# The relative-position bias of a two-layer encoder: one small DRAM copy read as overlapping rows, in place of 128 copies per head

## The chip, the cores and the metric

One core of a Trainium2 chip runs the whole program. The metric is device time in microseconds (us) of one execution; lower is better. TensorE (PE in the rows) multiplies matrices, with weight loads shown apart as PEld; VectorE is DVE, ScalarE (the activation engine) is ACT, GpSimd is POOL, and SyncE (SP) issues DMAs. ACT can issue DMAs too: a DMA issued by SP goes to the queue q1 of the profile, one issued by ACT to q10, and both are served by the core's 16 DMA engines.

## The reference, cut to what matters

Layer 0 is differential attention with a T5 relative-position bias and a block-causal mask; layer 1 is forgetting attention; both are followed by a squared-ReLU MLP (256 tokens, 2048 features, float32). The change concerns only the bias of layer 0:

```
rel  = key_pos[None, :] - q_pos[:, None]                  # [128 queries of a block, 256 keys]
bias = transpose(rel_table[t5_bucket(rel)], (2, 0, 1))    # 8 heads
mask = (key_pos[None, :] // 64) <= (q_pos[:, None] // 64)
s    = where(mask, s * scale + bias[None, :, None], -1e30)
p    = softmax(s)
```

The bias depends on the head and on key minus query alone. For the 256 queries and keys there are 383 such differences that the kernel needs (-255 to 127), so a head's bias is one row of 383 numbers, and each query reads a stretch of 256 of them, shifted by one from query to query.

## The kernel before

All products are float32 done as three reduced products: a weight tile `raw` is split into a high part `whi` (a cast on ACT, L171) and a low part `wlo` (a subtraction on VectorE, L174), and PE multiplies both with split operands. The weights come as *granules* of 512 KB, numbered here 0, 1, 2, ... in the order in which PE takes them. One granule is one *slot* of PE: about 2.8 us of matmuls. SP loads granules (L163) into four `raw` buffers; the load of granule i + 4 is issued when the low part of granule i has been taken. Five `whi` and five `wlo` buffers hold what is split, four granules ahead of PE. Each engine runs its instructions strictly in the order in which the program writes them, slot by slot: lists `pre`, `mid` and `post` say what side work stands in which slot.

The first eight slots (granules 0 to 7) make the first value block (L185 to L187), while x is still coming in; slots 8 to 11 make the queries of head 0, slots 12 to 15 its keys (L200, L203), and its scores follow two slots later. In the steady part one granule is taken in each slot.

The bias is made beside this. In slot 5 PE multiplies the table with a one-hot matrix from the host (`bias_rows`, L329) into `bp`: 8 heads by 383 differences. At the start of slot 6 VectorE copies it to `bs` (8 partitions, L333), and SP writes it to DRAM as `F` (L335), each head's row 128 times, 1532 KB in all. In slot 8 SP reads it back (L343) as `T`: 128 query rows by 8 heads by 256 keys, 1024 KB, by reading rows of 383 with a step of 382, so that each query's row begins one number earlier. GpSimd then writes the mask into a corner of `T` (L344). VectorE reads `T` in the softmax of each head (L406):

```
F = dr.tile([NA, P, NREL], F32, tag="F", name="F")
nc.sync.dma_start(out=F, in_=bs[:, 0:NREL].unsqueeze(1).broadcast_to([NA, P, NREL]))
...
src = src.rearrange("h (q r) -> q h r", r=NREL - 1)[:, :, 0:S]
nc.sync.dma_start(out=T, in_=src)
```

The DMA that reads `F` may be issued only once all of `F` has landed; SP waits for that, and its later loads wait behind it.

Of the kernel before, what the change touches and what calls it, by code (L numbers as in the profile page):

```python
# [11 lines left out]
F32 = mybir.dt.float32  # L12
# [8 lines left out]
P = 128  # L21
D = 2048
S = 256
HD = 128
FF = 8192
NA = 8          # differential heads
NF = 16         # forgetting heads
CW = 512        # columns of a token-major unit
# [6 lines left out]
NREL = 383      # rel = -255 .. 127  # L35

LA = 4          # granules split ahead of the products
NRAW = 4        # granules in flight from DRAM
# [4 lines left out]
def kernel(ctx: ExitStack, tc: tile.TileContext, *args):  # L43
# [11 lines left out]
    # ------------------------------------------------------------------ constants  # L55
# [9 lines left out]
    # 1 where a token is up to another: within a block of 128, and a block before  # L65
# [6 lines left out]
    # residual stream, token-major, by chunks of 512 features  # L72
# [6 lines left out]
    # the activation engine's tables come in beside the first loads  # L79
# [3 lines left out]
    # gains as columns: rows of 128 features, transposed  # L83
# [38 lines left out]
    # ------------------------------------------------------------------ the stream of weights  # L122
    # side work by slot of the tensor engine: before its weights' split, amid it, and after the products
    pre, mid, post = (defaultdict(list) for _ in range(3))
    order = []      # (unit, granule, token tiles): what the tensor engine does

    class Gran:
        """Weights of one transfer: kk tiles of 128 rows, 1024 numbers a partition."""
# [4 lines left out]
    class Unit:  # L133
        """One result in two banks: its granules, its operand, and what takes it."""
# [10 lines left out]
    def unit_b(W, r0, nk, c0, xs, done):  # L145
        """[256, 512] = x . W[r0 : r0 + nk * 128, c0 : c0 + 512], token-major."""
        gs = []
        for k in range(0, nk, 2):
            src = W[r0 + k * P:r0 + (k + 2) * P, c0:c0 + CW].rearrange("(k p) c -> p k c", p=P)
            gs.append(Gran(src, 2))  # L150
        return Unit("B", gs, xs, done)

    def unit_a(W, c0, xs, done):
        """[256 features, 256 tokens] = (x . W[:, c0 : c0 + 256]) transposed."""
        gs = []
        for k in range(0, 16, 4):
            src = W[k * P:(k + 4) * P, c0:c0 + 256].rearrange("(k p) c -> p k c", p=P)
            gs.append(Gran(src, 4))
        return Unit("A", gs, xs, done)
# [52 lines left out]
    # ------------------------------------------------------------------ pieces  # L212
    def new_x(tag):
        """Two 128-row tiles of an operand: high parts of 256 tokens, then low parts."""
        return sb.tile([P, 2, 2 * S], F32R, tag=tag, name=tag)

    def turn(c, tps):
        """h[c] feature-major, into two banks."""
        for b in range(2):
            for j in range(2):  # L220
                for m in range(2):
                    f = (2 * b + j) * P
                    nc.tensor.transpose(tps[b][:, (j * 2 + m) * P:(j * 2 + m + 1) * P],  # L223
                                        h[c][:, m, f:f + P], ident)

    def split_turned(c, tps, gain, dst, bs=(0, 1)):
        """High and low parts of gain . h[c] turned, from two pieces of 512 columns."""
        at = [(b, j, 4 * c + 2 * b + j) for b in bs for j in range(2)]
        for b, j, k in at:
            nc.scalar.activation(out=dst[2 * c + b][:, j, 0:S], in_=tps[b][:, j * S:(j + 1) * S],  # L230
                                 func=AF.Copy, scale=gain[:, k:k + 1])
        for b, j, k in at:
            nc.vector.scalar_tensor_tensor(out=dst[2 * c + b][:, j, S:2 * S], in0=tps[b][:, j * S:(j + 1) * S],  # L233
                                           scalar=gain[:, k:k + 1], in1=dst[2 * c + b][:, j, 0:S],
                                           op0=ALU.mult, op1=ALU.subtract)
# [10 lines left out]
    def rsqrt(ssum, n, scale, eps, name, bufs=1):  # L246
        """(ssum * scale + eps) ** -0.5 by columns: three Newton steps from the exponent's half."""
        v = sb.tile([P, n], F32, tag="rs_v", bufs=2, name="rs_v")
        w = sb.tile([P, n], F32, tag="rs_w", bufs=2, name="rs_w")
        t = sb.tile([P, n], F32, tag="rs_t", bufs=2, name="rs_t")  # L250
        y = sb.tile([P, n], F32, tag=name, bufs=bufs, name=name)
        nc.vector.tensor_scalar(out=v, in0=ssum, scalar1=scale, scalar2=eps, op0=ALU.mult, op1=ALU.add)
        nc.vector.tensor_scalar(out=y.bitcast(I32), in0=v.bitcast(I32), scalar1=-0.5,
                                scalar2=1597463007.0, op0=ALU.mult, op1=ALU.add)
        nc.vector.tensor_scalar(out=w, in0=v, scalar1=-0.5, scalar2=None, op0=ALU.mult)
        for _ in range(3):
            for i in range(n):
                c = slice(i, i + 1)
                nc.vector.scalar_tensor_tensor(out=t[:, c], in0=y[:, c], scalar=w[:, c], in1=y[:, c],
                                               op0=ALU.mult, op1=ALU.mult)  # L260
            for i in range(n):
                c = slice(i, i + 1)
                nc.vector.scalar_tensor_tensor(out=y[:, c], in0=t[:, c], scalar=1.5, in1=y[:, c],
                                               op0=ALU.add, op1=ALU.mult)
        return y

    class Norm:
        """Row statistics of the residual stream: rstd by token, and along the free axis."""
# [33 lines left out]
    def pair_sum(u):  # L302
        """The two halves of a feature-major unit's banks added: [128, 2, 256]."""
# [16 lines left out]
    # ------------------------------------------------------------------ prologue: x, T5 bias, lambda  # L320
# [10 lines left out]
    def bias_out():  # L331
        bs = sb.tile([NA, 512], F32, tag="e", bufs=2, name="bs")
        nc.vector.tensor_copy(out=bs[:, 0:NREL], in_=bias["p"][0:NA, 0:NREL])  # L333
        F = dr.tile([NA, P, NREL], F32, tag="F", name="F")
        nc.sync.dma_start(out=F, in_=bs[:, 0:NREL].unsqueeze(1).broadcast_to([NA, P, NREL]))  # L335
        bias["F"] = F

    def bias_in():
        T = sb.tile([P, NA, S], F32, tag="tnc", bufs=2, name="T")
        # T[q, head, j] = F[head, q, 127 - q + j]: rows of 383, read 382 apart  # L340
        src = bias["F"].rearrange("h q r -> h (q r)")[:, 127:127 + P * (NREL - 1)]
        src = src.rearrange("h (q r) -> q h r", r=NREL - 1)[:, :, 0:S]
        nc.sync.dma_start(out=T, in_=src)  # L343
        nc.gpsimd.memset(T[0:64, :, 192:256], NEG)  # L344
        bias["T"] = T

    def build_lambda():
# [7 lines left out]
        # -(e1 - e2 + init)  # L355
# [4 lines left out]
    # ------------------------------------------------------------------ layer 0: differential attention  # L360
# [25 lines left out]
    def diff_head(hd):  # L386
# [13 lines left out]
        def softmax(qt):  # L400
            def run():
# [3 lines left out]
                b = bias["T"][:, hd, S - nk:S].unsqueeze(1).broadcast_to([P, 2, nk])  # L405
# [96 lines left out]
    # boundary after the last product that a chunk of h takes  # L502
# [35 lines left out]
    n_mlp0, n_att1, n_mlp1 = (Norm.__new__(Norm) for _ in range(3))      # started by their first chunk  # L538
# [9 lines left out]
    def wo(W, kind, p0, p1, dones):  # L548
        """h += o . W over the head pairs p0 to p1; the last pair of the first two chunks comes last."""
# [13 lines left out]
    # ------------------------------------------------------------------ squared-ReLU MLP  # L563
    HX = {}

    def mlp(l, norm, key, last, start=None):
        for q in range(4):
# [20 lines left out]
            for c in range(NCH):  # L588
                u = unit_b(w_out[l], q * D, 16, c * CW, lambda hk=hk: HX[hk], adds[c] if q < 3 else last[c])
                if l == 1 and q == 3 and c == NCH - 1:  # L590
                    # the last result: one token tile ends before the other
# [8 lines left out]
    # ------------------------------------------------------------------ layer 1: forgetting attention  # L600
    fg = {}

    def gates(s0):
# [24 lines left out]
        def gate1():  # L628
            # z = logits by token; n = min(z, 0); t = exp(-|z|)
# [15 lines left out]
        def gate2():  # L645
            # log1p(t) = 2 atanh(s), s = t / (2 + t) in [0, 1/3]
# [20 lines left out]
        def gate4():  # L667
            # log sigmoid = min(z, 0) - log1p(exp(-|z|))
# [6 lines left out]
        def sums():  # L675
            # over the tokens up to each: by head and token
# [41 lines left out]
    def spread_c(g):  # L718
        """-c over the keys on every partition, causal on the diagonal blocks: diagonal 0 | full | diagonal 1."""
# [9 lines left out]
    def fox_pair(g, i):  # L729
        """Heads 4 g + 2 i and the next."""  # L730
# [88 lines left out]
    def v_first(s0):  # L819
        """Beside the first unit of layer 1: the forget gates, and the query operand."""  # L820
# [12 lines left out]
    def qkv_f(g):  # L833
# [6 lines left out]
        for i in range(2):  # L840
# [3 lines left out]
            def then(e, plan=plan, i=i):  # L844
                # the last values come after the last queries
# [16 lines left out]
    # ------------------------------------------------------------------ last MLP and the final norm  # L862
# [45 lines left out]
    # ------------------------------------------------------------------ emission  # L908
    grs, at = [], []        # the granules as they come; how many the slots so far have taken
# [22 lines left out]
    # the tensor engine's clock comes up while the first rows are on their way  # L932
# [42 lines left out]
    for s in range(n + 2):  # L975
        for f in pre.pop(s, []):
            f()
        # while x comes in, one granule less is split ahead
# [32 lines left out]
def bucket_onehot():  # L1011
    """Row b, column r: 1 where the T5 bucket of rel = r - 255 is b."""
    rel = np.arange(-255, NREL - 255)
# [29 lines left out]
```

## Time and profile before

| | us |
|---|---|
| median of 3 runs (lowest, highest) | 2267.74 (2267.03 to 2269.26) |
| span of the profiled execution, first to last instruction | 2266.5 |
| median less that span | 1.24 |
| PE busy | 2234.6 (99% of the span) |
| VectorE, ACT busy | 1356.8 (60%), 1022.4 (45%) |
| mean granted TensorE clock | 0.994 of full speed |

The profile gives the profiled execution by its span alone; what lies around it is taken as the 1.24 us between that span and the median. PE is busy nearly always, so the time of this kernel is PE's work plus PE's few idle stretches. A busy share over the whole span says little of a stage: the questions are when PE stands still, and what it then waits for.

### The profile page before, as it was taken

Reading aid. Unit: us, or ns where it says so; the run is one execution under the profiler, and the core shown is the slowest. Engines: PE = TensorE matmul, PEld = TensorE weight load, DVE = VectorE, ACT = ScalarE, POOL = GpSimd, SP = SyncE. Lnnn points to the kernel's source line nnn. Section 1 sums busy time; section 2 is a strip of 40 time slices with the busy share of each in tenths; the row PEclk is TensorE's granted clock in tenths of the full one; section 3 lists DMA queues with packets and bytes.
Section 4 is the critical chain, followed back from the end, with each engine's and each line's share of the span. In section 5 each row is a group of like instructions: output and inputs, shape, how many; then the busy total and the mean of one; then the engine's idle time right before and its main releaser. Section 6 shows DMA issues by size and latency. Waiting matters only on the chain.

```text
span 2266.5 us, 28986 instructions
## 1 busy us (share of the span) xinstructions
PE 2234.6 (99%) x11272; PEld 1874.0 (83%) x11272; DVE 1356.8 (60%) x1768; ACT 1022.4 (45%) x1343; POOL 14.0 (1%) x19
## 2 busy tenths in 40 slices
PE   8799999999999999999999999999999999999998
PEld 6688888888888888888888888888888888888886
DVE  4566665665565565466576556656645655655655
ACT  4454554443444344344554444454434434433443
POOL 0000000000000000000001000000000000000000
PEclk9899999999999999999999999999999999999999
DMA  7655555556556655666556565556565565565563
GB/s 198 200 178 176 159 176 177 171 187 200 180 187 194 191 184 188 187 189 188 170 169 203 175 192 181 178 168 203 186 187 185 186 194 178 186 197 178 187 200 130
DMA packets 319332, 416.06 MB, mean 184 GB/s; under 512 B 15066, under 2 KB 218972, under 8 KB 319068
## 3 DMA queue, kind: packets, MB, share of 16 engines
q1 hardware_dynamic: 319148, 414.20, 58.4%
q8 instruction: 88, 1.44, 0.3%
q14 instruction: 48, 0.39, 0.1%
q10 hardware_dynamic: 48, 0.02, 0.0%
HBM read 410.49 MB, written 3.68 MB: 183 GB/s over the span
## 4 chain that ended last, share of the span: by engine, by line
PE 97%; DMA 2%; DVE 0%; ACT 0%; issue 0%; SPq 0%; DVEq 0%; ACTq 0%
PE acc L200 31%; PE acc L203 16%; PE acc L187 15%; PE acc L185 15%; PE acc L186 15%; DMA raw<-in_w_qkv_a 2%; PE tp L223 1%; PE sc L396 0%; PE sc L739 0%; PE sc L187 0%; PE sc L186 0%; PE sc L185 0%; PE o L797 0%; PE fp L610 0%; PE o L798 0%; PE tpo L474 0%
## 5 line engine op out<-in xcount | busy, mean ns | idle before, releaser
L174 DVE TENSOR_TENSOR wlo<-raw,whi 128x1024 fp32r<-128x1024 f32 x767 | 926.1, 1224 | 646.9 <-ACT whi L171 646.1
L171 ACT CAST whi<-raw 128x1024 fp32r<-128x1024 f32 x767 | 797.3, 1050 | 751.5 <-PE acc L187 460.2
L200 PE MATMUL acc<-x,whi 128*128 128x512 f32 x2816 | 993.8, 399 | 18.7 <-ACT whi L171 18.7
L203 PE MATMUL acc<-x,wlo 128*128 128x256 f32 x2816 | 776.9, 281 | 0.5 <-DVE wlo L174 0.5
L200 PEld LDWEIGHTS acc<-x,whi 128*128 128x128 f32 x2816 | 525.5, 188 | 139.4 <-ACT whi L171 19.0
L203 PEld LDWEIGHTS acc<-x,wlo 128*128 128x128 f32 x2816 | 532.7, 189 | 9.1 <-DVE wlo L174 1.0
L185 PE MATMUL acc<-whi,hx 128*128 128x512 f32 x1120 | 443.4, 396 | 0.0
L187 PE MATMUL acc<-whi,hx 128*128 128x512 f32 x1120 | 442.4, 395 | 0.0
L186 PE MATMUL acc<-wlo,hx 128*128 128x512 f32 x1120 | 442.3, 395 | 0.0
L187 PEld LDWEIGHTS acc<-whi,hx 128*128 128x128 f32 x1120 | 209.9, 187 | 51.3
L186 PEld LDWEIGHTS acc<-wlo,hx 128*128 128x128 f32 x1120 | 210.0, 187 | 51.0
L185 PEld LDWEIGHTS acc<-whi,hx 128*128 128x128 f32 x1120 | 210.0, 187 | 50.5
L307 DVE TENSOR_TENSOR zs<-acc,z 128x512 f32<-128x512 f32 x96 | 66.3, 691 | 102.8 <-ACT z L306 102.8
L306 ACT COPY z<-acc 128x512 f32<-128x512 f32 x96 | 56.4, 587 | 157.1 <-PE acc L200 157.1
L581 ACT CAST hx<-s 128x512 fp32r<-128x512 f32 x64 | 39.8, 622 | 143.2 <-DVE s L579 143.2
L185 PE MATMUL acc<-whi,x 128*128 128x512 f32 x256 | 102.7, 401 | 0.2 <-ACT x L230 0.2
L187 PE MATMUL acc<-whi,x 128*128 128x512 f32 x256 | 100.1, 391 | 0.6 <-DVE x L233 0.6
L186 PE MATMUL acc<-wlo,x 128*128 128x512 f32 x256 | 99.8, 390 | 0.0
L200 PE MATMUL acc<-hx,whi 128*128 128x512 f32 x256 | 92.1, 400 | 0.0
L582 DVE TENSOR_TENSOR hx<-s,hx 128x512 fp32r<-128x512 f32 x64 | 44.3, 693 | 44.0 <-ACT hx L581 44.0
L203 PE MATMUL acc<-hx,wlo 128*128 128x256 f32 x256 | 70.6, 281 | 0.0
L318 DVE TENSOR_TENSOR h<-acc,h 128x512 f32<-128x512 f32 x88 | 56.7, 686 | 17.9 <-PE acc L187 17.8
(172 smaller groups left out, 1170.0 us busy)
## 6 DMA issues: line engine op xcount, KB each, us to landing
raw<-in_w_mlp_in SPq DMA_DIRECT2D x256, 512.0 KB, 3.9
raw<-in_w_mlp_out SPq DMA_DIRECT2D x256, 512.0 KB, 3.8
raw<-in_w_qkv_a SPq DMA_DIRECT2D x96, 512.0 KB, 4.6
raw<-in_w_o_a SPq DMA_DIRECT2D x32, 512.0 KB, 4.2
raw<-in_w_v_b SPq DMA_DIRECT2D x32, 512.0 KB, 3.8
raw<-in_w_k_b SPq DMA_DIRECT2D x32, 512.0 KB, 3.7
raw<-in_w_q_b SPq DMA_DIRECT2D x32, 512.0 KB, 3.8
raw<-in_w_o_b SPq DMA_DIRECT2D x32, 512.0 KB, 3.6
```

Source lines behind the costliest of these rows:

```text
L171: nc.scalar.copy(out=g.hi, in_=g.raw)
L174: nc.vector.tensor_tensor(out=g.lo, in0=g.raw, in1=g.hi, op=ALU.subtract)
L185: nc.tensor.matmul(bank[m], xh, hi[:, j, :], start=k == 0, stop=False)
L186: nc.tensor.matmul(bank[m], xh, lo[:, j, :], start=False, stop=False)
L187: nc.tensor.matmul(bank[m], xl, hi[:, j, :], start=False, stop=k == nk - 1)
L200: nc.tensor.matmul(bank[n], hi[:, j, w], xt, start=k == 0, stop=k == 15)
L203: nc.tensor.matmul(bank[n][:, 0:S], lo[:, j, w], xt[:, 0:S], start=False, stop=False)
L306: nc.scalar.copy(out=z1, in_=u.acc[:, :, S:2 * S])
L307: nc.vector.tensor_tensor(out=zs, in0=u.acc[:, :, 0:S], in1=z1, op=ALU.add)
L318: nc.vector.tensor_tensor(out=h[c][:, m, :], in0=u.bank[m], in1=h[c][:, m, :], op=ALU.add)
L581: nc.scalar.copy(out=t[:, :, 0:S], in_=s)
L582: nc.vector.tensor_tensor(out=t[:, :, S:2 * S], in0=s, in1=t[:, :, 0:S], op=ALU.subtract)
```

## The change

`F` holds each head's row once (8 by 383), with the differences in reversed order, 127 down to -255. It is written by a DMA that ACT issues. `T` is read back, also on ACT's queue, with the step 1 from partition to partition: partition q reads 256 numbers from place q of each head's row, so the rows overlap. What partition q then holds is its bias with the keys in reversed order; VectorE reads it with step -1, and the mask's corner moves from the last 64 columns to the first 64. The one-hot matrix from the host has its columns reversed to suit. The rest of the diff removes comments.

```
     def bias_out():
         bs = sb.tile([NA, 512], F32, tag="e", bufs=2, name="bs")
         nc.vector.tensor_copy(out=bs[:, 0:NREL], in_=bias["p"][0:NA, 0:NREL])
-        F = dr.tile([NA, P, NREL], F32, tag="F", name="F")
-        nc.sync.dma_start(out=F, in_=bs[:, 0:NREL].unsqueeze(1).broadcast_to([NA, P, NREL]))
+        F = dr.tile([NA, NREL], F32, tag="F", name="F")
+        nc.scalar.dma_start(out=F, in_=bs[:, 0:NREL])
         bias["F"] = F

     def bias_in():
         T = sb.tile([P, NA, S], F32, tag="tnc", bufs=2, name="T")
-        src = bias["F"].rearrange("h q r -> h (q r)")[:, 127:127 + P * (NREL - 1)]
-        src = src.rearrange("h (q r) -> q h r", r=NREL - 1)[:, :, 0:S]
-        nc.sync.dma_start(out=T, in_=src)
-        nc.gpsimd.memset(T[0:64, :, 192:256], NEG)
+        F = bias["F"]
+        src = bass.AP(F.tensor, F.offset, [[1, P], [NREL, NA], [1, S]])
+        nc.scalar.dma_start(out=T, in_=src)
+        nc.gpsimd.memset(T[0:64, :, 0:64], NEG)
         bias["T"] = T
...
-                b = bias["T"][:, hd, S - nk:S].unsqueeze(1).broadcast_to([P, 2, nk])
+                b = bias["T"][:, hd, 0:nk][:, ::-1].unsqueeze(1).broadcast_to([P, 2, nk])
...
-    rel = np.arange(-255, NREL - 255)
+    rel = np.arange(127, 127 - NREL, -1)
```

On SP's queue, at slots 6 to 8, this is what stood and what stands (- before, + after). `raw_323` is granule 12, `raw_363` granule 13, `raw_405` granule 14 and so on; a name like DMAHW6 is the semaphore of an earlier DMA.

```order
 L163 DMA raw_323<-in_w_qkv_a 128x4x256 [waits DMAHW5_49,DVE_49]
-L335 DMA F_357<-bs_355 1024x1x383 [waits DMAHW6_49,DVE_49]
 L163 DMA raw_363<-in_w_qkv_a 128x4x256 [waits DMAHW7_49,DMAHW2_49,DVE_49]
-L163 DMA raw_405<-in_w_qkv_a 128x4x256 [waits DMAHW3_49,DMAHW0_49,DVE_49]
-L343 DMA T_428<-F_357 128x8x256 [waits DMAHW6_49,DMAHW1_49]
+L163 DMA raw_405<-in_w_qkv_a 128x4x256 [waits DMAHW3_49,DMAHW1_49,DVE_49]
 L163 DMA raw_438<-in_w_qkv_a 128x4x256 [waits DMAHW4_49,DVE_49]
 L163 DMA raw_441<-in_w_qkv_a 128x4x256 [waits DMAHW5_49,DVE_49]
```

Both bias transfers have left SP's queue: the loads of granules 13 and 14 no longer stand behind the write of `F`, and those from granule 15 on no longer behind the wait for `F`.

On ACT, in slots 6 to 8, the two transfers stand in the line of the casts. `whi_359` and `whi_377` are the casts of granules 9 and 10, `whi_431` and `whi_434` those of 11 and 12, `junk` the squares of x, `v` the first value block.

```order
 L243 ACTIVATE junk_353,stat_95<-h3_81 128x512 [waits Activation_49]
-L171 CAST whi_359<-raw_233 128x1024 [waits DMAHW2_49,DVE_49]
-L171 CAST whi_377<-raw_269 128x1024 [waits DMAHW3_49,DVE_49,PE_49]
+L335 DMA F_357<-bs_355 8x383 [waits DMAHW6_49,DVE_49]
+L171 CAST whi_359<-raw_233 128x1024 [waits DMAHW2_49]
+L171 CAST whi_377<-raw_269 128x1024 [waits DMAHW3_49,PE_49]
 L371 ACTIVATE v_423<-acc_169,rstd_385 128x512 [waits DVE_49,PE_49]
 L371 ACTIVATE v_423<-acc_169,rstd_385 128x512 [waits DVE_49]
 L958 CAST wfs_93<-wf_raw_91 128x16x16 [waits DMAHW0_49]
+L343 DMA T_428<-F_357 128x8x256 [waits DMAHW6_49]
 L171 CAST whi_431<-raw_287 128x1024 [waits DMAHW4_49]
 L171 CAST whi_434<-raw_323 128x1024 [waits DMAHW5_49]
```

The write of `F` now stands ahead of the cast of granule 9, and the read of `T`, with its wait for `F` (DMAHW6), ahead of the cast of granule 11. PE, VectorE and GpSimd have the same instructions in the same order as before.

## Rows read from the trace of the kernel before

**Rows 1.** The page, part 1: busy time, share, instructions of each engine.

```profile
PE 2234.6 (99%) x11272; PEld 1874.0 (83%) x11272; DVE 1356.8 (60%) x1768; ACT 1022.4 (45%) x1343; POOL 14.0 (1%) x19
```

**Rows 2.** Waits of PE from 28 us to the end: total, times, longest (us).

```profile
PE acc L200 <- ACT whi L171: 18.7, 1, 18.7
PE acc L203 <- DVE wlo L174: 0.5, 1, 0.5
```

**Rows 3.** The critical chain between 30 and 75 us: start, length, what.

```profile
35.34 31.23 DMA raw<-in_w_qkv_a
```

**Rows 4.** Timeline of SP (DMA issues): start, length, line, transfer, count.

```profile
29.18 0.82 SPq L335 DMA_DIRECT2D F<-bs  x1
35.34 14.60 SPq L163 DMA_DIRECT2D raw<-in_w_qkv_a  x2
65.21 0.37 SPq L343 DMA_DIRECT2D T<-F  x1
```

**Rows 5.** Stretches: length, busy of each engine (instructions), clock, DMA share, GB/s.

```profile
33.00:36.00 3.00, 3.00 (x16) 2.29 (x15) 1.81 (x6) 2.00 (x4) 0.00 (x0) 1.00 0.97 313
56.00:60.00 4.00, 0.00 (x0) 0.00 (x0) 0.00 (x0) 0.00 (x0) 0.00 (x0) 0.50 0.47 50
```

**Rows 6.** Timeline of PE: start, length, line, operation, idle before it.

```profile
35.17 0.40 PE L200 MATMUL acc<-x,whi 128*128 128x512 f32 x1
...
37.99 0.40 PE L200 MATMUL acc<-x,whi 128*128 128x512 f32 x1
...
43.57 0.27 PE L203 MATMUL acc<-x,wlo 128*128 128x256 f32 x1
...
48.55 0.39 PE L200 MATMUL acc<-x,whi 128*128 128x512 f32 x1
...
67.75 0.80 PE L200 MATMUL acc<-x,whi 128*128 128x512 f32 x1 [18.69 <-ACT whi L171]
...
73.23 0.47 PE L200 MATMUL acc<-x,whi 128*128 128x512 f32 x1
...
97.28 0.27 PE L434 MATMUL tpa<-ident,e 128*128 128x128 f32 x1
```

**Rows 7.** Timeline of ACT, same columns.

```profile
33.02 1.98 ACT L171 CAST whi<-raw 128x1024 fp32r<-128x1024 f32 x2
37.32 1.27 ACT L371 ACTIVATE v<-acc,rstd 128x512 f32<-128x512 f32 x2 [2.32 <-DVE rstd L263]
...
38.77 2.00 ACT L171 CAST whi<-raw 128x1024 fp32r<-128x1024 f32 x2
```

**Rows 8.** Timeline of VectorE, same columns.

```profile
34.09 1.23 DVE L174 TENSOR_TENSOR wlo<-raw,whi 128x1024 fp32r<-128x1024 f32 x1 [4.93 <-ACT whi L171]
...
37.73 1.22 DVE L174 TENSOR_TENSOR wlo<-raw,whi 128x1024 fp32r<-128x1024 f32 x1
...
39.86 2.36 DVE L174 TENSOR_TENSOR wlo<-raw,whi 128x1024 fp32r<-128x1024 f32 x2 [0.25 <-ACT whi L171]
...
94.86 0.48 DVE L427 SCALAR_TENSOR_TENSOR e<-e,rr 128x256 f32<-128x256 f32 x1
```

**Rows 9.** Transfers of 1188 to 1196 us: issues, KB, us to landing.

```profile
NC<-C SPq DMA_DIRECT2D x1, 512.0 KB, 7.3
...
C<-fg_nc SPq DMA_DIRECT2D x1, 16.0 KB, 4.9
```

**Rows 10.** Transfers of 60 to 66.3 and of 1538 to 1550 us, same columns.

```profile
raw<-in_w_qkv_a SPq DMA_DIRECT2D x1, 512.0 KB, 6.4
...
gf<-in_final_norm_g SPq DMA_DIRECT2D x1, 1024.0 KB, 6.8
```

**Rows 11.** A DMA issued by ACT, and GpSimd's wait for T (timelines).

```profile
0.98 0.38 ACTq L85 DMA_DIRECT2D grow<-in_attn_norm_g  x1
...
70.65 0.52 POOL L344 MEMSET T<- 64x512 f32 x1 [68.14 <-DMA T<-F]
```

**Rows 12.** Busy time of L406, the reader of T, in a stretch.

```profile
40.00:340.00 300.00, 8.83 (x16) 0.97 0.58 173
```

## Prediction

> **What bounds the kernel now.** I read the busy times first, then PE's waits, then the chain of waits at the one place where PE stands still, then SP's timeline there. PE is busy for 99% of the span [rows 1], so only an idle stretch of PE, or work of PE done slowly, can be won or lost. From 28 us to the end PE has two waits in all: one of 18.7 us for a cast, and right behind it one of 0.5 us for the low part of the same granule [rows 2]. There is nothing else to win there, and a new wait on another engine costs something only if it grows to reach PE.
>
> The long wait lies between the matmuls at 48.55 and 67.75 us [rows 6]. PE has used up granule 12 and waits for granule 13. The chain says why: the load of granule 13, issued at 35.34, landed 31.23 us later [rows 3]. SP's timeline names what stood ahead of it: at 29.18 the write of F, 1532 KB, was issued, and the two loads after it went into the same queue behind it; SP then stood until 65.21 before it could issue the read of T, which needs all of F [rows 4]. The stretches show that this is no lack of DMA capacity: up to 36 us the 16 engines are 0.97 busy at 313 GB/s, but in the middle of the write they are 0.47 busy at 50 GB/s [rows 5]. The backlog of loads drained until about 36 us, and from there to 65.2 us F trickled out through about half of the engines; at 56 to 60 us PE, VectorE and ACT did nothing at all. So the cause of PE's wait is the long write of F and the loads behind it; it is not the read of T, and no engine's work.
>
> **What the stall costs.** In an undisturbed stretch eight pairs of matmuls take 37.99 - 35.17 = 2.82 us, 0.3525 us a pair [rows 6]. From the last pair before the stall (48.55) to the first at the old pace after it (73.23) there are eight steps too, which took 24.68 us. The stall costs 24.68 - 2.82 = 21.86 us. [...]
>
> **The change, part by part.**
>
> *The write of F shrinks from 1024 rows of 1532 bytes to 8, and leaves SP's queue.* Removed: all that stands ahead of granule 13. Its load, issued near 35.5, then finds only T beside it.
>
> *ACT issues F.* bs is ready before ACT gets there, since SP could issue F at 29.18, while ACT is at the cast of granule 9 only at 33.02 [rows 4, 7]. The one issue by ACT in the trace took 0.38 us, SP's issue of the big F 0.82 us [rows 4, 11]; I take 0.5 us for each issue (bounds 0.38 and 0.82). F's issue moves the cast of granule 9, its low part, the row statistics and the v block behind them by 0.5 us.
>
> *ACT issues T, and waits for F.* With that shift ACT comes to T at 38.77 + 0.5 = 39.3 us, 6.3 us after F's issue began at 33.0 [rows 7]. How long does a write of 8 rows take to land? The nearest row is the small write C, 16 rows of 1 KB to DRAM with loads beside it: 4.9 us [rows 9]. The other bound is the old F, about 36 us from issue to landing, but for 128 times the rows [rows 4]. Between ends so far apart I take the row that it is most like, C: F lands near 38.4, so ACT does not wait. [...]
>
> *What is queued behind these two issues?* The casts of granules 11 and 12, at 38.77 before, now at 38.77 + 1.0 = 39.8. The low part of granule 11 began at 39.86 and ended at about 41.1 (half of 2.36 us) [rows 8], and now ends at 42.1. PE takes it at 43.57, the second matmul of slot 11 [rows 6]. So there is a cover of some 1.4 us: it carries the two issues at 0.5 us each (0.9 us if both cost 0.82 us), and **from there on every microsecond that F lands after about 40.7 costs one**. This is the tightest place of the change.
>
> *T beside the loads.* T is still 1 MB, now from about 39.8 on. Before, it was issued at 65.21 and had landed at 70.65, when GpSimd could write into it: 5.4 us [rows 4, 11]. The load issued right behind it landed in 6.4 us [rows 10]. The load of granule 14 goes out when the low part of granule 10 is done, at 37.73 + 1.22 + 0.5 = 39.5 us [rows 8]. PE wants granule 13 at 48.55 + 0.35 = 48.9 and granule 14 a slot later, 51.7; less a cast and a low part (1.0 + 1.2 us), granule 14 must land by 49.5, 10 us after its issue. At 6.4 us it is there 3.6 us early; granules 15 and 16, issued at about 42.2 and 43.4, have until 52.3 and 55.1. Granule 13 has more still. So T is hidden. New is that T reads its megabyte from 12 KB of DRAM, each number up to 128 times. Two rows are like it: gf reads one row of 8 KB into 128 partitions, 1 MB, in 6.8 us, and NC reads 4 KB 128 times, 512 KB, in 7.3 us with loads beside it [rows 9, 10]. Both near the price of fresh data, so I take 5.4 to 7.3 us. The upper bound is F's pace: 1024 rows in 29.2 us on about 7.5 engines (0.47 of 16) is 0.21 us a row and engine; T at that pace on 16 engines would take 64 x 0.21 = 13.6 us, which is a rival below.
>
> [...]
>
> *VectorE reads T backwards.* The 16 instructions at L406 take 8.83 us in all [rows 12]. No row shows a backward read. Bounds: nothing, or a doubling, 0.55 us each. Between the last of head 0's weights (94.86 + 0.48 = 95.34) and PE's transpose of them (97.28) lie 1.9 us [rows 6, 8]; both reads of a head doubled are 1.1 us. So either bound costs PE nothing; without that cover it would be up to 8.8 us. I take nothing. The memset on GpSimd is of the same size.
>
> **The sum.** Gone: 21.86 us. Added on the path: 0. The span becomes 2266.5 - 21.9 = 2244.6 us. The median lies 1.24 us above the span, so the time becomes 2267.74 - 21.86 = **2245.9 us**, 1.0% less.
>
> **The rivals.**
>
> *F lands late (12%).* Up to 36 us the engines are full of loads [rows 5]. If F waits for that backlog and then takes C's 4.9 us, it lands at 40.9, 0.2 us too late; some 3 us more of issue cost and landing would put PE's wait at up to 3 us: 2246 to 2249 us. For it speaks the small cover; against it, that F has a queue of its own.
>
> *T is slow (8%).* At 0.21 us a row, taking turns with rows of the loads (1 MB of two loads, 64 rows an engine, at 313 GB/s over 16 engines 0.05 us each, 3.3 us), T ends near 39.8 + 13.6 + 3.3 = 56.7, and so does granule 15, wanted by 52.3: a stall of 4.4 us, with up to 3 us of slow clock behind it: 2250 to 2253 us. Against it speak gf and NC.
>
> *Slower than before (2%).* ACT runs in order, and its wait for F holds every cast. If the write's time lay not in its 1024 rows but in something that eight rows keep, ACT would stand from 39.3 until F lands; a landing after 40.7 + 21.9 - 3.0 = 59.6 us (26 us after issue, with the same 3 us of slow clock) brings no gain, and the old 36 us would give a time about 9 us above the old one, 2277. Against it: 26 us for 8 rows, with C's 16 rows in 4.9.
>
> *The stall stays (3%).* If the loads were late for a reason of their own, taking F away would leave 2267. The stretch before F shows the same loads at 313 GB/s, so I see none.
>
> **The numbers.** The likeliest, with 75%, is 2245.9, by itself 2245.2 to 2247.4: the runs of before scatter from -0.7 to +1.5 us about their median. The range that should hold 8 in 10 reaches into the late F, 2244.5 to 2250. A change of 0.2%, 4.5 us, is about what a measurement can tell from none. Faster by more: 0.95 (the likeliest and the first two rivals); within it 0.03; slower 0.02.
>
> **What would show it.** Right: PE with no wait near 49 us, a clock of 1.00 through 75 us, F landing in about 5 us on ACT's queue, T in 5 to 7 us, the load of granule 13 in 4 to 7 us, the cast of granule 11 at about 39.8, L406 at 8.8 us in all. Wrong: an ACT wait at L343 for F beyond 40.7, with PE idle at about 43; loads of granules 14 and 15 landing more than 10 us after their issue; or PE waiting for a transpose of a head because L406 has grown.

## The result, and the profile after

The changed kernel takes 2246.77 us (median of 4 runs, 2246.13 to 2247.36), beside 2268.43 us of the kernel before on the same chip: a ratio of 0.9907 with a 95% interval of 0.9893 to 0.9921, 21.66 us less. Forecast were 2245.9 us and 21.86 us less.

The page of the changed kernel, its span and part 1, and the rows of the two queues from part 3 (packets, MB, share of 16 engines):

```profile
span 2245.5 us, 28983 instructions
PE 2233.2 (99%) x11272; PEld 1874.0 (83%) x11272; DVE 1358.0 (60%) x1768; ACT 1022.7 (46%) x1343; POOL 13.4 (1%) x19
q1 hardware_dynamic: 317076, 411.59, 58.3%
q10 hardware_dynamic: 1104, 1.08, 0.2%
```

PE's busy time has hardly moved (2234.6 before, [rows 1]); the span has shrunk around it. Asked for PE's waits from 28 us to the end, the view that gave [rows 2] now has no row at all. The stretches that answer to [rows 5]:

```profile
33.00:36.00 3.00, 3.00 (x15) 2.22 (x14) 1.01 (x1) 2.87 (x6) 0.00 (x0) 1.00 1.04 343
56.00:60.00 4.00, 4.00 (x25) 3.53 (x24) 3.48 (x5) 1.99 (x3) 0.00 (x0) 1.00 0.82 253
```

At 56 to 60 us PE is busy throughout at a granted clock of 1.00, and the DMA engines move 253 GB/s where they moved 50. The timeline of ACT, to be held against [rows 7], shows both bias DMAs in their new place (ACTq rows are issues):

```profile
33.29 0.63 ACT L243 ACTIVATE junk<-h 128x512 f32<-128x512 f32 x1
33.35 0.51 ACTq L335 DMA_DIRECT2D F<-bs  x1
33.83 0.19 ACT L243 ACTIVATION_READ_ACCUMULATOR junk<-h 128x1 f32 x1
33.92 1.98 ACT L171 CAST whi<-raw 128x1024 fp32r<-128x1024 f32 x2
38.22 0.69 ACT L371 ACTIVATE v<-acc,rstd 128x512 f32<-128x512 f32 x1 [2.32 <-DVE rstd L263]
38.62 0.40 ACTq L343 DMA_DIRECT2D T<-F  x1
38.80 0.68 ACT L371 ACTIVATE v<-acc,rstd 128x512 f32<-128x512 f32 x1
39.37 0.41 ACT L958 CAST wfs<-wf_raw 128x256 fp32r<-128x256 f32 x1
39.67 2.96 ACT L171 CAST whi<-raw 128x1024 fp32r<-128x1024 f32 x3
46.72 1.05 ACT L171 CAST whi<-raw 128x1024 fp32r<-128x1024 f32 x1 [4.09 <-DMA raw<-in_w_qkv_a]
```

Two things are to be seen. In this execution everything from about 28 us on runs 0.9 us later than in the trace before (the matmuls of slot 6 begin at 29.40 us, against 28.50). The casts of granules 9 and 11, at 33.92 and 39.67 against 33.02 and 38.77, are later by these 0.9 us and no more. So the two issues cost ACT nothing: each went out while an activation still ran (33.35 beside the one from 33.29, 38.62 beside the one from 38.22). And no cast waits for F. Granule 13 is cast in the group of three at 39.67 without a wait. Granule 14, whose load took some 7 us from its issue at 39.87, is cast at 46.72; PE needs it at 52.6.

GpSimd's wait for T and the reader of T, as in [rows 11, 12]:

```profile
45.44 0.52 POOL L344 MEMSET T<- 64x512 f32 x1 [42.93 <-DMA T<-F]
40.00:340.00 300.00, 8.84 (x16) 1.00 0.57 178
```

T was issued at 38.62 and had landed at 45.44, 6.8 us. The 16 backward reads take 8.84 us, the forward ones took 8.83.

### The profile page after: what moved, and what is told of

Its sections match the earlier page's. It is cut to its first block, busy times and chain, and to the rows that moved or that the text cites. A ratio compares the mean times of both kernels' runs of the same rounds, so it can differ in the third digit from the quotient of the medians.

```text
span 2245.5 us, 28983 instructions
## 1 busy us (share of the span) xinstructions
PE 2233.2 (99%) x11272; PEld 1874.0 (83%) x11272; DVE 1358.0 (60%) x1768; ACT 1022.7 (46%) x1343; POOL 13.4 (1%) x19
## 4 chain that ended last, share of the span: by engine, by line
PE 99%; DMA 0%; DVE 0%; ACT 0%; SPq 0%; issue 0%; DVEq 0%; ACTq 0%
PE acc L200 32%; PE acc L203 16%; PE acc L185 16%; PE acc L187 16%; PE acc L186 16%; PE tp L223 1%; PE sc L396 0%; PE sc L739 0%; PE sc L187 0%; PE sc L186 0%; PE sc L185 0%; PE o L797 0%; DMA h<-in_x 0%; PE fp L610 0%; PE o L798 0%; PE tpo L474 0%
```

## The experiments

Each was timed beside the kernel before, which gave 2267.6 to 2267.9 us; in brackets behind a time stand its ratio to that and the 95% interval. The lines with - and + are against the changed kernel, in "Old F" and "Rows of 1536 bytes" against the kernel before. Where a run has an extra write F2, nothing reads it.

**Small F, both DMAs on SP's queue.** Is it the size of F or the queue?

```
-        nc.scalar.dma_start(out=F, in_=bs[:, 0:NREL])
+        nc.sync.dma_start(out=F, in_=bs[:, 0:NREL])
...
-        nc.scalar.dma_start(out=T, in_=src)
+        nc.sync.dma_start(out=T, in_=src)
```

> The changed kernel with both bias DMAs put back on SP's queue; F stays 8 rows. My theory (the 1024 slow rows of F ahead of the loads are the whole cause, the queue does not matter): F's eight rows pass quickly, SP does not stand at the read of T, PE has no wait near 49 us, 2245.5 to 2248 us, within 0.1% of the changed kernel's 2246.8. Rival (the move to ACT's queue is what gains): the loads again wait behind F, 2260 to 2268 us. Third (SP's wait for F to land costs a few us by itself): a PE wait of 1 to 5 us, 2248 to 2252.

Measured 2246.74 us (0.9907, 0.9892 to 0.9922), and PE again has no wait after 28 us. SP's timeline:

```profile
29.89 0.58 SPq L335 DMA_DIRECT2D F<-bs  x1
36.04 4.00 SPq L163 DMA_DIRECT2D raw<-in_w_qkv_a  x2
40.13 0.46 SPq L343 DMA_DIRECT2D T<-F  x1
```

Against [rows 4], T goes out 25 us sooner and SP does not stand for F. The move to ACT's queue is worth nothing here; the size of F is worth all of it.

**Old F, both DMAs on ACT's queue.** The other half alone.

```
-        nc.sync.dma_start(out=F, in_=bs[:, 0:NREL].unsqueeze(1).broadcast_to([NA, P, NREL]))
+        nc.scalar.dma_start(out=F, in_=bs[:, 0:NREL].unsqueeze(1).broadcast_to([NA, P, NREL]))
...
-        nc.sync.dma_start(out=T, in_=src)
+        nc.scalar.dma_start(out=T, in_=src)
```

> The kernel before with both bias DMAs moved to ACT's queue; F stays 1024 rows of 1532 bytes. My theory: ACT runs in order and stands at the read of T until F has landed; F needs some 29 us of its own, so it lands at 63 to 69 us, the cast of granule 11 comes then, PE waits from about 44 us: 2270 to 2278 us, slower than the kernel before (2268.4). Rival (moving the transfers off SP's queue gains by itself): 2247 to 2256 us. The loads of granules 13 and 14 show what F costs a load when F is in the other queue: 6 to 10 us to landing if they take turns, about 30 if they still stand behind it.

Measured 2274.51 us (1.003, 1.0019 to 1.0041): slower than before. Of the waits (total, times, longest) of PE from 28 us on and of ACT between 28 and 100 us, and the load that SP issued between 34 and 38 us (KB, us to landing):

```profile
PE acc L200 <- ACT whi L171: 24.4, 1, 24.4
...
ACT whi L171 <- DMA F<-bs: 27.1, 1, 27.1
...
raw<-in_w_qkv_a SPq DMA_DIRECT2D x1, 512.0 KB, 23.5
```

This is what the prediction's rival "Slower than before" describes: ACT stands at the read of T until F has landed, and every cast behind it waits. The load of granule 13, now in another queue than F, still took 23.5 us, not the 6 to 10 of taking turns; when granule 14's landed, the trace does not show.

**An extra write of F's old form, on ACT's queue behind T.** Does a queue of its own protect the loads when nothing waits for the write?

```
         nc.scalar.dma_start(out=T, in_=src)
+        F2 = dr.tile([NA, P, NREL], F32, tag="F2", name="F2")
+        nc.scalar.dma_start(out=F2, in_=h[0][0:NA, 0, 0:NREL].unsqueeze(1).broadcast_to([NA, P, NREL]))
```

> The changed kernel with an extra write of 1024 rows of 1532 bytes from 8 partitions (a stretch of x, in F's old form) on ACT's queue right behind the read of T; nothing reads it. If the 16 DMA engines are what matters (rows of the write and of the loads take turns on the 8 engines that the write uses, 0.21 us a row): each load takes about 8 us beside it, one load in 8 us where PE takes one in 2.8, so over the 30 us of the write 6 to 7 loads are missing, of which 3 to 4 are covered by what is split and landed: PE waits 5 to 15 us, 2252 to 2264 us. If a separate queue is enough: no PE wait, 2246 to 2248 us.

Measured 2263.41 us (0.9984, 0.9974 to 0.9993), at the upper end of the first theory. PE's waits from 28 us on:

```profile
PE acc L200 <- ACT whi L171: 8.4, 2, 6.4
PE acc L203 <- DVE wlo L174: 1.6, 3, 0.8
PE sc L398 <- DVE k L313: 1.4, 1, 1.4
```

These are 11.4 us; the rest of the 16.6 us by which this run is slower than the changed kernel is put down to work at the lower clock (0.50 to 0.83 in the stretches from 56 to 76 us). The casts of granules 14, 15 and 16 came at 49.49, 59.99 and 68.27 us, one in 8 to 10 us, near the theory's one load in 8. So most of the old loss, 16.6 of 21.7 us, comes back with no wait for F and no load behind the write in its queue: the write takes the engines' time itself. Between 36 and 100 us ACT's queue took 24.6% of the time of the 16 engines, T's read included.

**The same write on SP's queue at F's old place.**

```
         nc.scalar.dma_start(out=F, in_=bs[:, 0:NREL])
+        F2 = dr.tile([NA, P, NREL], F32, tag="F2", name="F2")
+        nc.sync.dma_start(out=F2, in_=h[0][0:NA, 0, 0:NREL].unsqueeze(1).broadcast_to([NA, P, NREL]))
```

> The changed kernel with the same extra write of 1024 rows on SP's queue, at the place where F's write stood before; nothing reads it or waits for it, and F and T go their new way on ACT's queue. My theory (order within the queue holds the loads): the load of granule 13 lands about 30 us after its issue, PE waits 15 to 20 us from about 49 us, 2263 to 2269 us, close to the kernel before. Rival (SP's wait at the read of T, 15.2 us, was the cost): with that wait gone the loads land in time or a few us late, 2247 to 2253 us.

Measured 2269.25 us (1.0006, 0.9997 to 1.0016), as slow as the kernel before. But the loss is made up otherwise than expected: PE waits twice, 5.69 us until 49.14 and 10.77 us until 68.36. The first wait is for a cast that stands behind ACT's wait for F, the second for granule 13. The load of granule 13 in the chain, ACT's waits and the landing of T:

```profile
35.30 31.88 DMA raw<-in_w_qkv_a
...
ACT whi L171 <- DMA raw<-in_w_qkv_a: 20.8, 5, 17.2
ACT whi L171 <- DMA F<-bs: 9.2, 1, 9.2
...
T<-F ACTq DMA_DIRECT2D x1, 1024.0 KB, 21.7
```

Granule 13 landed 31.88 us after its issue, as before (31.23, [rows 3]), though SP no longer waits at the read of T: that wait was not what held it. The eight rows of F, alone in ACT's queue, took 15 us beside the write in the other queue (issued at 32.41, T issued at 47.60): the rival "F lands late", in a case where something crowds it.

**Rows of 1536 bytes.** Why is the write slow? First guess: its odd row length.

```
-NREL = 383      # rel = -255 .. 127
+NREL = 384      # rel = -255 .. 127
```

> The kernel before with rows of F of 384 numbers in place of 383 (1536 bytes, a multiple of 512, so that every row of F starts at such a multiple in DRAM); all else as before. Theory that a row's price is per row and engine, whatever its length: F still takes about 29 us from 36 us on, 2267 to 2270 us. Rival (rows of 1532 bytes that start off a boundary are what makes the write slow): F lands at 42 to 50 us, the stall of PE shrinks to less than 5 us, 2247 to 2253 us.

Measured 2267.52 us (0.9999, 0.999 to 1.0009): no difference in time. In the chain, F takes 34.54 us from issue to landing; before, SP came past its wait for F 36 us after the issue [rows 4]. The rival, a landing at 42 to 50 us, is out.

**The extra write from 128 partitions, behind T.** Same bytes, same rows in DRAM.

```
+        F2 = dr.tile([P, NA, NREL], F32, tag="F2", name="F2")
+        nc.scalar.dma_start(out=F2, in_=h[0][:, 0, 0:NREL].unsqueeze(1).broadcast_to([P, NA, NREL]))
```

> The changed kernel with an extra write of the same bytes as in the run with 8 partitions, 1024 rows of 1532 bytes into one stretch of DRAM, behind the read of T on ACT's queue, but read from all 128 partitions (8 rows each), so that 16 engines carry it; nothing reads it. If a row costs 0.21 us of an engine whatever its source: 64 rows an engine, 13.6 us alone and some 18 beside loads. If the slowness comes of eight partitions being read 128 times each: 4 to 7 us, no PE wait, 2246 to 2248 us. By the first, PE waits 0 to 4 us, 2246 to 2251 us.

Measured 2250.67 us (0.9925, 0.9908 to 0.9941): 12.7 us better than from 8 partitions, with waits of PE of 2.6 us in all. It landed in 16.0 us, in the same stretch as T and four loads, so this run could not separate a price per row from plain sharing; the runs below could.

**T read one slot earlier.** How long do eight rows take to land?

```
-    pre[8].append(bias_in)
+    pre[7].append(bias_in)
```

> The changed kernel with the read of T in slot 7 in place of slot 8, ahead of ACT's cast of granule 10. ACT then comes to it at about 35.5 us, 2 us after the issue of F, and must wait: the time of T's issue shows when F has landed. By the prediction's term (4.9 us, from the small write C): T is issued at about 38 us, granule 10 is cast 3 us later than before, still in time for its slot at 41.4: 2246 to 2249 us. [...] By the rival that F waits for the loads on the engines: T issued after 40, PE waits 1 us or more before slot 10.

Measured 2246.54 us (0.9908, 0.9893 to 0.9922). ACT's timeline:

```profile
33.70 0.51 ACTq L335 DMA_DIRECT2D F<-bs  x1
...
36.54 0.45 ACTq L343 DMA_DIRECT2D T<-F  x1
37.09 1.05 ACT L171 CAST whi<-raw 128x1024 fp32r<-128x1024 f32 x1 [1.79 <-DMA F<-bs]
```

ACT waited, and T went out 2.8 us after the issue of F: that is F's landing. The row of C, 4.9 us, was too high for it.

**Five late writes.** The same 1532 KB once more, in slot 30 (99 us), long after T, with one load in 2.8 us beside them. Only the source's partitions differ; the lengths of the middle dimension follow.

```
+    def extra_out():
+        F2 = dr.tile([128, 8, NREL], F32, tag="F2", name="F2")
+        nc.scalar.dma_start(out=F2, in_=h[0][0:128, 0, 0:NREL].unsqueeze(1).broadcast_to([128, 8, NREL]))
+    pre[30].append(extra_out)
```

The other sources are `0:16` (64 rows each), `0:8` (128 rows each), `0:96:12` (8 partitions, 128 rows each) and `0:128:8` (16 partitions, 64 rows each).

> The changed kernel with an extra write of 1024 rows of 1532 bytes (a stretch of x, unread) on ACT's queue in slot 30, long after T, when one load in 2.8 us is all the traffic; source 128 partitions of 8 rows, 16 engines. If a written row costs 0.21 us of its engine: 64 x 0.21 = 13.6 us alone, 16 us or more to landing, PE waits up to 5 us. If rows from many partitions move at the rate of the loads: 6 to 10 us to landing, no PE wait, 2246 to 2248 us.

> The same extra write in slot 30 with the source in 16 partitions of 64 rows each: again 16 engines and 64 rows an engine, but each partition is read 64 times. If the repeated reading of one partition is what costs 0.21 us a row: about 13.6 us alone, 15 to 20 us to landing, loads beside it late, 2247 to 2254 us. If it is only that 8 engines carry the write: like the one from 128 partitions, 6 to 10 us, 2246 to 2248 us.

> The same extra write in slot 30 with the source in 8 partitions of 128 rows each, F's old form: 8 engines. By the 29 us that F took: 27 us or more to landing, loads beside it 8 us and more each, PE waits 5 to 17 us: 2252 to 2264 us, as in the run with this write in slot 8. If a write so late were covered (more granules landed by then): less than 5 us of waits, below 2252.

> The extra write in slot 30 with the source in 8 partitions again, 128 rows each on 8 engines, but 12 partitions apart (0, 12, ..., 84) in place of 0 to 7. If one partition read over and over is what costs 0.21 us a row: as with partitions 0 to 7, about 30 us to landing, PE waits 5 to 15 us, 2252 to 2262 us. [...]

> The extra write in slot 30 with the source in 16 partitions, 64 rows each on 16 engines, 8 partitions apart (0, 8, ..., 120) in place of 0 to 15. If one partition read over and over is what costs: 17 to 19 us to landing as with partitions 0 to 15, 0.2 us a row. [...] Either way 2246 to 2249 us, since the write from partitions 0 to 15 cost PE nothing.

The row of ACT's queue between 88 and 140 us (packets, MB, share of 16 engines) in the five runs, in the order 128 partitions; 0 to 15; 0 to 7; 8 apart by 12; 16 apart by 8:

```profile
q10 hardware_dynamic: 1040, 1.57, 12.5%
```

```profile
q10 hardware_dynamic: 1040, 1.57, 25.3%
```

```profile
q10 hardware_dynamic: 1032, 1.57, 25.5%
```

```profile
q10 hardware_dynamic: 1032, 1.57, 8.7%
```

```profile
q10 hardware_dynamic: 1040, 1.57, 12.4%
```

Beyond the 1024 rows there are 8 packets with eight source partitions, and 16 with 16 or 128. The author's estimate takes them as one an engine, so 8 and 16 engines. The old F on ACT's queue agrees with the 8: alone between 40 and 42 us, it took 46.7% of the 16 engines, 7.5 of them. Where the landing is known, the share spread over the time from issue to landing makes 8.8 engines (128 partitions), 11.8 (0 to 15) and 9.2 (16 apart), above 8 each time; that there were 16 is not shown. The share times 16 engines times 52 us, divided by the packets, is what one row costs its engine:

| source partitions | engine time a row, us | issue to landing, us | PE's waits, us | median, us |
|---|---|---|---|---|
| 0 to 127 | 0.10 | 11.8 | 0 | 2246.74 |
| 0 to 15 | 0.20 | 17.9 | 0 | 2246.59 |
| 0 to 7 | 0.21 | not shown | 7.3 | 2256.04 |
| 0, 12, ..., 84 | 0.07 | not shown | 0 | 2246.95 |
| 0, 8, ..., 120 | 0.10 | 11.2 | 0 | 2246.75 |

Eight partitions that each give 128 rows are the cheapest a row when they lie apart (0.07 us), and the dearest when they lie side by side (0.21 us). So neither the 128 readings of one partition nor the 8 engines is the cause: it is where the partitions lie. With 16 partitions it is the same: 0.20 us a row side by side, 0.10 us when they lie 8 apart. The theories did not all hold: the write from 128 partitions fits neither of its two (0.10 us a row, 11.8 us to landing), and the one from 0 to 15 landed as its first theory says, but cost no time. Why rows out of neighbouring partitions cost more, no run here shows, nor why a row out of 128 partitions, or out of 16 that lie apart, costs 0.10 us where one out of eight that lie apart costs 0.07.

With partitions 0 to 7 PE waits 7.3 us in slot 30 (in the profiled execution, which took 2258.84 us) and 11.4 us in slot 8, where T shares the engines too; whether that makes the difference is not shown. The four others cost nothing that the runs can tell. The waits of the write from partitions 0 to 7 in slot 30:

```profile
PE acc L200 <- ACT whi L171: 6.1, 2, 4.0
PE acc L203 <- DVE wlo L174: 1.2, 2, 0.8
```

## Why the prediction was right

*The stall and its price.* 21.86 us were read off the trace; 21.66 went. The 21.86 us have two parts: 18.85 us of idle time (from 48.55 to 67.75, less a step of 0.35), and 3.01 us in the seven steps from 67.75 to 73.23, which took 5.48 us where seven take 2.47 [rows 6]. The granted clock there was 0.50, as the trace before shows between 66 and 70 us:

```profile
66.00:70.00 4.00, 1.79 (x4) 1.18 (x5) 2.27 (x3) 2.09 (x2) 0.00 (x0) 0.50 0.95 300
```

These 3.01 us are the 3 us of slow clock in the rivals. Not all of them were slow work: PE's second wait, of 0.5 us, lies in them [rows 2]. Both parts went together: as forecast, PE has no wait, and the granted clock is 1.00 in every stretch from 33 to 76 us.

*The cause.* That the write of F and not the read of T or SP's wait held the loads is shown by the small F on SP (all of the gain without the move) and by the extra write on SP: with F small and T elsewhere granule 13 again lands 31.88 us after its issue. That run's time says less, since 5.69 us of PE's waits there are behind ACT's wait for F. SP was held ahead of that wait already: its two issues of loads behind F took 14.60 us in all [rows 4], where one takes 0.37 us now. What was not seen is that order within SP's queue is only part of it: in the other queue the same write costs 16.6 us too. "No lack of DMA capacity" was read off a mean over 16 engines; 0.47 of them is 7.5 engines, nearly all of the 8 at which the packets put a write of this form.

*The issues on ACT.* Sized at 0.5 us each, they took 0.51 and 0.40 us and cost nothing, since they ran beside an activation.

*F's landing.* Sized at 4.9 us from C, it measured 2.8 us, in the run with T one slot earlier. The cover before a late F costs time was therefore not 2.3 us (38.4 against 40.7) but more than 5 us: F, issued at 33.35 in the trace after, landed near 36.2, and the limit of 40.7 is 41.6 there, with the 0.9 us by which this execution runs later. The error was on the safe side, so the sum did not feel it. "F lands late" was given 12%; crowded by a second write it happens, in this kernel it had more room than thought.

*T.* Sized at 5.4 to 7.3 us, it measured 6.8 us, and granule 14's load some 7 us against the 6.4 assumed: it is hidden. Reading 12 KB of DRAM 85 times over on average cost PE nothing: it has no wait after 28 us. The bound for the rival "T is slow", F's 0.21 us a row, was the wrong price for it: that price belongs to a source of eight neighbouring partitions, and T's source is DRAM.

*The backward read.* Taken as nothing; 0.01 us in all (8.84 against 8.83).

*What lies between 2245.9 and 2246.77.* The forecast span of 2244.6 agrees with the four executions (2244.2 to 2245.5 us); their device time is some 1.9 us above the span (2247.36 for 2245.5), where 1.24 was taken from the median of other executions.

## What to carry to other kernels

Before moving a transfer to another queue, find out what it takes from the engines: here a slow write delayed the loads from either queue (granule 13 landed 31.23 us after its issue with F in the same queue, 23.5 us with F in the other), and what helped was to make the write smaller or faster. A write of 1024 rows out of eight neighbouring partitions moved 50 GB/s in the stretch from 56 to 60 us, where the loads had moved 313; spreading the same rows over eight partitions that lie apart cut the engine time of a row to a third, from 0.21 to 0.07 us. And look at what stands behind a DMA that must wait for another DMA: the wait for F held SP, and the loads behind it, for 15.2 us in one version, and ACT, with its casts, for 27.1 us in another.

## What the runs showed that was not expected

A write of 1024 rows took 0.21 us of an engine per row from partitions 0 to 7 and 0.07 us from eight partitions 12 apart. Beside the old F on ACT's queue a load in the other queue, that of granule 13, took 23.5 us, where the author's estimate for rows taking turns was 6 to 10 us; beside the extra write on ACT's queue casts came 8 to 10 us apart. How the engines share their time between the two queues was not settled.
